# A decoder layer with routed experts: overflow code without branches, its loop moved, and expert matrices laid out in 16 KB rows

## The chip, the cores and the metric

The kernel runs on one core of one Trainium2 chip. The metric is the device time of one execution in microseconds (us). Of the core's parts, five matter here. PE (TensorE) multiplies matrices. DVE (VectorE) and ACT (ScalarE) do elementwise work, and they alone bring results from PE's accumulators (PSUM) to the on-chip memory (SBUF). SP (SyncE) issues nearly all loads from the chip's main memory (HBM), in the order of the program, on one queue that sixteen DMA engines serve. An instruction that has to wait on an engine or on SP holds back all that stand behind it there. POOL (GpSimd) does hardly anything in the part that is told of.

## What is computed

One decoder layer on 256 tokens of 1024 channels, all in float32: token mixers, a cross-attention, and then experts, each followed by a layer norm. The change touches the experts. A router gives each token its best 4 of 32 experts, with weights; each expert is a pair of matrices, w1 (1024 x 2048) and w2 (1024 x 1024):

```python
h = x_pad[tok] @ w1[e] + b1[e]
h_gate, h_up = h[:, :EXPERT_FF], h[:, EXPERT_FF:]
h_gate = jnp.minimum(h_gate, SWIGLU_LIMIT)
h_up = jnp.clip(h_up, -SWIGLU_LIMIT, SWIGLU_LIMIT)
act = h_gate * jax.nn.sigmoid(SWIGLU_ALPHA * h_gate) * (h_up + 1.0)
y = (act @ w2[e] + b2[e]).astype(F32)
return acc.at[tok].add(y * gate[:, None]), None
```

How many tokens an expert gets depends on the data. Every expert's 12 MB are used once, so all 403 MB are read in each execution.

## The kernel before, in words

The first third (mixers, cross-attention, router) is not touched. The experts follow, in 16 pairs; `prepare` (from line 1274) picks the tokens of a pair, CAP = 64 places for each expert, with matmuls against a selection (`gather`, line 1080: the tiles `xg1` to `xg15`, made one pair ahead, within the second expert of the pair before). Then, for each expert, in the order of the program on PE: w1 in four chunks (`expert_in`, line 1103), the activation on DVE and ACT (lines 1119 to 1123), four transposes (1130, 1131), w2 in two chunks (`expert_out`, 1144). After the second expert of a pair its results are added to the tokens (`add_out`, 1162 and 1163).

**The stream.** SP issues the chunks in the order in which they are used, six to an expert, 2 MB each (`echunk` and `fetch`, line 1023). They go to ten slots in turn (`RINGS`): a chunk can only be issued when PE is through with the chunk of ten places before. The names of the slots are tags of pools; one of them, `r3`, is the last of the ten. In memory an expert's matrices lie as they are given, row by row. A chunk of w1 is 256 rows of 8 KB and is loaded so that a partition takes two rows, p and p + 128; a chunk of w2 is 512 rows of 4 KB, of which a partition takes four. The matrices of the first third, `w_in`, are laid out by the host instead (in `layout`): each chunk as 128 partitions of 8 x 512 floats, 16 KB without a break.

**Overflow.** An expert may get more than 64 tokens. Before the experts start, the kernel looks for the expert with most tokens and swaps it with place PX = 17 (the order of the others stays; from place 2 on, SP reads from a table `idx_i` which expert's matrices to load). Places 65 to 96 of expert 17 are computed in a narrower form (`Extra`, 32 places, matmuls of 256 columns), with its matrices still in their slots: `overflow_in` behind its w1 and `overflow_out` behind its w2, each under a branch on the count (`tc.If`, line 1229 for the first) that PE, DVE and ACT read from the table `cnt_i`. Places beyond 96 have a loop within that branch. For all other experts stands `overflow_others` (from line 1237): if the highest count of the others is over 64, a loop over all experts loads matrices again, through POOL into slot `r3`, and computes the rest. It stands behind pair 8, that is behind expert 17, and all engines, SP too, load the count (line 1240) and take the branch (line 1241). In the data of these runs expert 17 has between 65 and 96 tokens, and no other has over 64: the first branch's work is done, the loop is skipped.

**The end.** Before expert 31, four accumulators are opened with the sum so far (`final`, line 1153), so that the last pair's results are added there; then the last layer norm, whose factors (`ln3`) SP loads behind all chunks, and four stores of the output.

Of the kernel before, what the change touches and what calls it, by code (L numbers as in the profile page):

```python
# [13 lines left out]
F32 = mybir.dt.float32  # L14
F32R = mybir.dt.float32r
BF16 = mybir.dt.bfloat16
I32 = mybir.dt.int32
U32 = mybir.dt.uint32
AF = mybir.ActivationFunctionType
OP = mybir.AluOpType  # L20
AX = mybir.AxisListType

P = 128
D = 1024
T = 256
NT = T // P
KT = D // P
E = 32
CAP = 64
# [4 lines left out]
NS = 2  # L34
PX = 17
# [12 lines left out]
def layer_kernel(ctx, tc, a, out, dbg=None):  # L48
    nc = tc.nc
# [954 lines left out]
    order = pool(ctx, "order")  # L1004

    Rp = order.tile([P, 2 * NT, E], F32, name="Rp")
    tab_i = order.tile([1, 2 * E + 2], I32, name="tab_i")
    cnt_i, idx_i = tab_i[:, 0:E + 2], tab_i[:, E + 2:]


    RINGS = [(ring2, "ring2")] * 3 + [(ring, "ring"), (ring3, "r0"), (ring3, "r1"), (ring, "ring"), (ring, "ring"),
# [3 lines left out]
    def slot(shape, name):  # L1015
        p, tag = RINGS[nslot[0] % len(RINGS)]
        nslot[0] += 1
        return p.tile(shape, F32, tag=tag, name=name)
# [10 lines left out]
            fetch(w[:, k:k + n], view[:, k:k + n])  # L1029
        return w  # L1030

    w1v = a["w_exp_in"][0].rearrange("e (c k p) n -> e c p k n", k=2, p=P)
    w2v = a["w_exp_out"][0].rearrange("e (c k p) n -> e c p k n", k=4, p=P)

    def of(v, e):
        return v[e] if isinstance(e, int) else v[bass.ds(e, 1)].rearrange("o c p k n -> (o c) p k n")
# [3 lines left out]

    def w2_views(e):
        return [([P, 4, D], of(w2v, e)[c]) for c in range(2)]

    BRANCH = (mybir.EngineType.PE, mybir.EngineType.DVE, mybir.EngineType.Activation)

    class Main:

# [11 lines left out]
    class Extra(Main):  # L1059
# [6 lines left out]
        bank = gate  # L1066
# [59 lines left out]
    def expert_turn(v, hu, at, nm):  # L1126
        W = v.W
        pt = v.bank("pt" + nm)
        for u in range(W // P):
            nc.tensor.transpose(pt[:, u * P:(u + 1) * P], hu[:, u * P:(u + 1) * P], ident)  # L1130
        nc.scalar.activation(at, pt[:, :W], AF.Copy, scale=0.5)  # L1131
# [18 lines left out]
    def final(t, half, alloc):  # L1150

        finals[t, half] = ps = alloc(f"pc{t}{half}_last")
        nc.tensor.matmul(ps, ident, acc[:, t, half * 512:half * 512 + 512], start=True, stop=False)

    def add_out(v, ct, y, rows, t, cols, nm):
        if finals:
# [48 lines left out]
    def extra_out(at, ct, w2, nm):  # L1205
        extra_add(expert_out(extra, at, w2, False, nm), ct, nm)
# [13 lines left out]
    def columns(e):  # L1220

        es = slice(e, e + 1)
        return Rp[:, 0:NT, es], Rp[:, NT:2 * NT, es], sel3p[:, es]

    def overflow_in(e, cnt, w1, w2):

        state = extra_tiles(f"x{e}")
        with tc.If(cnt > CAP):
            with tc.If(cnt > CAP + 32):
                for base in range(CAP + 32, T, 32):  # L1230
                    nm = f"x{e}_{base}"
                    extra_in(*columns(e), w1, base, *state, nm)
                    extra_out(*state, w2, nm)
            extra_in(*columns(e), w1, CAP, *state, f"x{e}")
        return state

    def overflow_others():

        pool = [mybir.EngineType.Pool]
        most = nc.values_load(cnt_i[0:1, E + 1:E + 2])  # L1240
        with tc.If(most > CAP):
            with tc.For_i(0, E) as i:
                here = bass.ds(i, 1)
                cnt = nc.values_load(cnt_i[0:1, here])
                with tc.If(cnt > CAP):
                    idx = nc.values_load(idx_i[0:1, here], engines=pool, min_val=0, max_val=E - 1)
                    own = md.tile([P, 2 * NT, 1], F32, tag="own", bufs=1, name="own")
                    sel = md.tile([3 * E, 1], BF16, tag="ownsel", bufs=1, name="ownsel")
                    nc.vector.tensor_copy(own, Rp[:, 0:2 * NT, here])
                    nc.vector.tensor_copy(sel, sel3p[:, here])  # L1250

                    def again(nm, shape, view):
                        w = ring3.tile(shape, F32, tag="r3", name="again" + nm)
                        nc.gpsimd.dma_start(w, view)
                        return w

                    def block(base):
                        nm = f"z{base}"
                        state = extra_tiles(nm)
                        extra_in(own[:, 0:NT], own[:, NT:], sel, (again(nm, s, w) for s, w in w1_views(idx)), base,  # L1260
                                 *state, nm)
                        py = expert_out(extra, state[0], (again(nm, s, w) for s, w in w2_views(idx)), False, nm)
                        extra_add(py, state[1], nm)

                    block(CAP)
                    with tc.If(cnt > CAP + 32):
                        for base in range(CAP + 32, T, 32):
                            block(base)

    def overflow_out(e, cnt, state, w2):  # L1270
        with tc.If(cnt > CAP):
            extra_out(*state, w2, f"x{e}")

    def prepare(pr):

# [55 lines left out]

    swap(few[0:1], few[0:1])
    nc.vector.tensor_copy(idx_i, few[0:1, 0])
    nc.vector.tensor_copy(cnt_i[0:1, E:E + 1], few[0:1, 1, PX:PX + 1])
    nc.vector.memset(few[0:1, 1, PX:PX + 1], 0.0)
    nc.vector.tensor_copy(cnt_i[0:1, 0:E], few[0:1, 1])
    nc.vector.tensor_reduce(kmax[0:1], few[0:1, 1], axis=AX.X, op=OP.max)
    nc.vector.tensor_copy(cnt_i[0:1, E + 1:E + 2], kmax[0:1])

# [22 lines left out]
    for pr in range(E // 2):  # L1364
        xg, og, rest = nxt
        Y = [md.tile([P, 512], F32, tag=f"Y{i}", bufs=1, name=f"Y{i}_{pr}") for i in range(2)]
        for i in range(2):
            e = 2 * pr + i
            w1 = []
            ex = e if e < NS else nc.values_load(idx_i[0:1, e:e + 1], engines=[mybir.EngineType.SP], min_val=0,  # L1370
                                                 max_val=E - 1)
            for c, (sh, view) in enumerate(w1_views(ex)):
                w1.append(echunk(sh, view, f"w1_{e}_{c}"))
                if e == 1 and c == 0:
                    acc_start(*acc_load())
            w2 = [echunk(sh, view, f"w2_{e}_{c}", 4 if e == E - 1 and c else 1)
                  for c, (sh, view) in enumerate(w2_views(ex))]
            nm = f"{e}"
            cnt = nc.values_load(cnt_i[0:1, E:E + 1], engines=BRANCH) if e == PX else None
            if e == E - 1:  # L1380
                for t, half in ((0, 0), (0, 1), (1, 0)):
                    final(t, half, bank)
            ps2 = expert_in(main, (sel3 if e < NS else sel3p)[:, e:e + 1], xg[:, :, i * CAP:(i + 1) * CAP], w1, nm, rest if e == 0 else None)
            hu = expert_swiglu(main, ps2, nm)
            if e == E - 1:
                final(1, 1, gbank)
            at = main.tile("at" + nm)
            state = overflow_in(e, cnt, w1, w2) if e == PX else None

            with tc.issue_after(nc.cur_bb.bb.instructions[-1]) if e == PX else ExitStack():  # L1390
                expert_turn(main, hu, at, nm)
            if i == 0:
                cts = [md.tile([P, T], F32, tag=f"ct{j}", bufs=1, name=f"ct{j}_{pr}") for j in range(2)]
                for j in range(2):
                    gate_rows(main, og[:, :, j:j + 2].rearrange("p t a s -> p t (a s)"), cts[j], f"{pr}_{j}")
            py = expert_out(main, at, w2, i == 1, nm)
            for j in range(2):
                rows = slice(j * CAP, (j + 1) * CAP)
                nc.scalar.activation(Y[j ^ i][rows, :], py[rows, :], AF.Copy)  # L1399
            if i == 1:  # L1400
                if pr + 1 < E // 2:
                    nxt = prepare(pr + 1)
            if e == PX:
                overflow_out(e, cnt, state, w2)
        for t in range(NT):
            for half in range(2):
                add_out(main, cts[half], Y[half], slice(0, P), t, slice(half * 512, half * 512 + 512), f"{half}_{pr}")

        if pr == PX // 2:
            overflow_others()  # L1410

    ln3 = slot([P, 2, D], "ln3")
    nc.sync.dma_start(ln3[:, 0], a["ln3_g"].to_broadcast([P, D]))
    nc.sync.dma_start(ln3[:, 1], a["ln3_b"].to_broadcast([P, D]))
    st = md.tile([P, NT, 2, 6], F32, tag="ln_st", bufs=1, name="ln3st")
    for t in range(NT):
        for half in range(2):
# [13 lines left out]
def masks():  # L1431
# [5 lines left out]
    def level(s):  # L1437
# [5 lines left out]


_PLAIN = ["x", "positions", "w_diff_o", "w_gdn_o", "w_mix_o", "ln1_g", "ln1_b", "w_cq", "w_ck", "w_cv", "w_co",
          "ln2_g", "ln2_b", "w_router", "b_router", "w_exp_in", "b_exp_in", "w_exp_out", "b_exp_out", "ln3_g",
          "ln3_b"]


def layout(inputs):  # L1450
# [3 lines left out]
    arr["memT"] = fm(np.asarray(inputs["mem"])[0], T)  # L1454
    arr["ln2_T"] = fm(np.concatenate([inputs["ln2_g"], inputs["ln2_b"]]), 2)
    arr["masks"] = masks()
    cw = np.asarray(inputs["gdn_conv_w"])[0]
    w = np.asarray(inputs["w_in"])[0]
    c = lambda o, g: np.arange(o + 256 * g, o + 256 * g + 256)
# [34 lines left out]
```

## Time and profile before

| what | value |
|---|---|
| median of 3 runs | 1528.34 us (1526.82 to 1529.77) |
| the profiled execution | 1527.18 us, of which its span in the profile 1525.5 us |
| PE busy | 1396.3 us, 92% of the span |
| DVE, ACT busy | 577.1 us (38%), 427.3 us (28%) |
| DMA | 480.21 MB in 91290 packets, 315 GB/s on average |

The page of the profile shows the share of busy time, the span in 40 slices, the DMA queues, the chain of work that ended last, and the costliest groups of instructions. Behind it stands the whole trace, which answers questions by line, tile, wait and stretch of time. An engine's "busy" for PE overlaps from one matmul to the next, so that 92% does not tell by itself whether PE is the bound; for that the waits are read. In the lists, "a <- b" after a wait means that a waited until b was done; names as PEq or SPq mean the engine's own queue of instructions; x16 is a count.

### The profile page before, as it was taken

The numbers are of one execution on the slowest core, as the hardware profiler recorded it, in microseconds if no ns is written. First come the engines' busy times: TensorE is split into PE (matmuls) and PEld (weight loads), VectorE is DVE, ScalarE is ACT, GpSimd is POOL, SyncE is SP. The second block draws the span as 40 slices with busy tenths as digits, with TensorE's granted clock in tenths as the row PEclk, the third lists the DMA queues.
The fourth block names the chain that finished last, engine by engine and source line by source line (L and its number), as shares of the span: only waits on it lengthen the run. The fifth ranks groups of instructions, "written<-read, shape, count | busy, mean of one in ns | idle before, by whom it ended". The sixth has DMA issues, their size and how long they took to land. (4 is left out here: it accounts for less than half of the span.)

```text
span 1525.5 us, 21509 instructions
## 1 busy us (share of the span) xinstructions
PE 1396.3 (92%) x8749; PEld 778.6 (51%) x8750; DVE 577.1 (38%) x1434; ACT 427.3 (28%) x925; POOL 8.8 (1%) x25
## 2 busy tenths in 40 slices
PE   7999999999999999999999999978689889899895
PEld 6788978799988633333333333323223323323331
DVE  6587869667875532112112112111112112112113
ACT  6575757665574311101101101100001101101111
POOL 0000000000000000000000000000000000000000
PEclk9999999999999999999999999997899999999998
DMA  7243334266854899999999999990799999999995
GB/s 278 96 167 112 111 112 148 75 225 206 304 215 159 318 404 418 418 416 416 418 418 416 417 417 418 416 389 2 291 418 417 418 415 418 418 417 415 418 418 219
DMA packets 91290, 480.21 MB, mean 315 GB/s; under 512 B 4336, under 2 KB 6928, under 8 KB 56144
## 3 DMA queue, kind: packets, MB, share of 16 engines
q1 hardware_dynamic: 90368, 475.72, 78.0%
q0 software_dynamic: 816, 3.04, 0.7%
q8 instruction: 71, 1.16, 0.3%
q14 instruction: 35, 0.29, 0.1%
HBM read 477.69 MB, written 1.05 MB: 314 GB/s over the span
## 5 line engine op out<-in xcount | busy, mean ns | idle before, releaser
L1103 PE MATMUL pgt<-w,xg 128*64 128x512 f32 x1024 | 250.6, 602 | 36.3 <-DMA w<-in_w_exp_in_dram 36.3
L1144 PE MATMUL py<-w,at 128*64 128x512 f32 x1024 | 242.5, 623 | 14.7 <-ACT at L1131 14.7
L1103 PE MATMUL pup<-w,xg 128*64 128x512 f32 x1024 | 248.6, 598 | 0.0
L1119 DVE TENSOR_SCALAR hg<-pgt 128x512 f32<-128x512 f32 x32 | 22.1, 692 | 511.4 <-PE pgt L1103 511.4
L1103 PEld LDWEIGHTS pgt<-w,xg 128*64 128x64 f32 x1024 | 71.6, 137 | 191.6 <-issue 135.3
L1103 PEld LDWEIGHTS pup<-w,xg 128*64 128x64 f32 x1024 | 75.6, 139 | 149.2 <-issue 149.2
L1120 ACT ACTIVATE th<-hg 128x512 f32<-128x512 f32 x32 | 20.1, 629 | 469.7 <-DVE hg L1119 469.7
L1144 PEld LDWEIGHTS py<-w,at 128*64 128x64 f32 x1024 | 72.2, 142 | 154.2 <-issue 129.7
L1399 ACT ACTIVATE Y<-py 64x512 f32<-64x512 f32 x64 | 37.9, 592 | 180.4 <-PE py L1144 180.0
L1162 PE MATMUL pc<-Y,ct 128*128 128x512 f32 x120 | 55.4, 604 | 2.7 <-ACT Y L1399 2.7
L1131 ACT ACTIVATE at<-pt 128x512 f32<-128x512 f32 x32 | 19.1, 597 | 94.9 <-PE pt L1130 94.9
L1163 DVE TENSOR_TENSOR acc<-acc,pc 128x512 f32<-128x512 f32 x60 | 41.1, 685 | 8.2 <-PE pc L1162 6.5
L1097 PEld LDWEIGHTS <-sel3p 96*64 96x64 bf16 (+1 forms) x128 | 10.5, 109 | 52.3 <-issue 52.3
L1097 PE MATMUL pup<-b,sel3p 96*64 96x512 bf16 x60 | 12.2, 389 | 25.4 <-DVE hu L1122 25.4
L1162 PEld LDWEIGHTS pc<-Y,ct 128*128 128x128 f32 x120 | 21.6, 189 | 26.9 <-issue 14.8
L334 DVE SCALAR_TENSOR_TENSOR u<-ps_g,feat,u 128x255 f32<-128x255 f32 (+2 forms) x72 | 33.1, 474 | 0.3
L1130 PE MATMUL pt<-ident,hu 128*128 128x128 f32 x128 | 21.5, 290 | 10.2 <-DVE hu L1123 10.2
L1121 DVE SCALAR_TENSOR_TENSOR hg<-th,hg 128x512 f32<-128x512 f32 x32 | 22.1, 692 | 22.3 <-ACT th L1120 22.3
L230 PE MATMUL ps_g<-xT,wg_0h 128*128 128x256 f32 x96 | 28.1, 293 | 0.9 <-ACT wg_0h L219 0.9
L232 PE MATMUL ps_g<-xT,wg_0l 128*128 128x256 f32 x96 | 28.1, 293 | 0.3 <-DVE wg_0l L220 0.3
L231 PE MATMUL ps_g<-xT,wg_0h 128*128 128x256 f32 x96 | 28.0, 292 | 0.0
L230 PE MATMUL ps_g<-xT,wg_1h 128*128 128x256 f32 x96 | 27.8, 290 | 0.0
(944 smaller groups left out, 2535.5 us busy)
## 6 DMA issues: line engine op xcount, KB each, us to landing
w<-in_w_exp_in_dram SPq DMA_DIRECT2D x128, 2048.0 KB, 25.8
w<-in_w_exp_out_dram SPq DMA_DIRECT2D x63, 2048.0 KB, 31.0
w_g<-in_w_in_dram SPq DMA_DIRECT2D x7, 2048.0 KB, 7.7
w_d<-in_w_in_dram SPq DMA_DIRECT2D x4, 2048.0 KB, 7.8
w_gt<-in_w_in_dram SPq DMA_DIRECT2D x4, 2048.0 KB, 7.8
w_dv<-in_w_in_dram SPq DMA_DIRECT2D x2, 2048.0 KB, 12.2
w_diffo<-in_w_diff_o_dram SPq DMA_DIRECT2D x2, 2048.0 KB, 11.7
w_gdno<-in_w_gdn_o_dram SPq DMA_DIRECT2D x2, 2048.0 KB, 8.3
```

The source lines that it names most:

```text
L230: nc.tensor.matmul(ps, h[:, kk, :], src[0][:, k, :], start=k == 0, stop=False)
L231: nc.tensor.matmul(ps, h[:, kk, :], src[1][:, k, :], start=False, stop=False)
L232: nc.tensor.matmul(ps, l[:, kk, :], src[0][:, k, :], start=False, stop=k == KT - 1)
L334: m1 = nc.vector.scalar_tensor_tensor(y[:, sh:], ps[:, :T - sh], convw[:, blk, tau:tau + 1], y[:, sh:], op0=OP.mult, op1=OP.add)
L1097: nc.tensor.matmul(ps[j * n:(j + 1) * n, :W], sel, b1[:, i * D + j * W:i * D + (j + 1) * W], start=True, stop=False)
L1103: nc.tensor.matmul(ps[j * n:(j + 1) * n, :W], xg[:, 2 * c + kk, :], w[:, kk, i * D + j * W:i * D + (j + 1) * W], start=False, stop=c == 3 ...
L1119: nc.vector.tensor_scalar(hg, pgt, 7.0, None, op0=OP.min)
L1121: nc.vector.scalar_tensor_tensor(hg, th, 1.0, hg, op0=OP.add, op1=OP.mult)
L1144: nc.tensor.matmul(py[j * n:(j + 1) * n, :W], at[:, k % U, (k // U) * n:(k // U + 1) * n], w[:, kk, hf * W:(hf + 1) * W], start=k == 0, st ...
L1162: nc.tensor.matmul(pc, ct[rows, t * P:(t + 1) * P], y[rows], start=True, stop=True)
L1163: nc.vector.tensor_tensor(acc[:, t, cols], acc[:, t, cols], pc, op=OP.add)
L1399: nc.scalar.activation(Y[j ^ i][rows, :], py[rows, :], AF.Copy)
```

## The change

Three things are done at once.

The overflow of expert 17 (`overflow_in`, and `extra_out` in place of `overflow_out`) is now always computed, for places 65 to 96, without a branch; the loads of its count on PE, DVE and ACT are gone. Places beyond 96 are left to the loop: the count of expert 17 in the table is set to 0 unless it is over 96, and positions up to 96 are cleared on DVE before the loop.

`overflow_others` is moved from behind pair 8 to just before the matmuls of expert 31, behind the issue of all chunks and of `ln3`, whose loads are moved up for that. Its loads go to the slot that is next in turn instead of `r3`, and its branch gets a new argument, `preferred_fallthrough_block=False`. The matmuls of expert 31 are held behind the opening of its accumulators.

The host lays `w_exp_in` and `w_exp_out` out so that in each chunk a partition's data is one run of 16 KB. The bytes and the slots of a chunk stay the same.

```diff
-    tab_i = order.tile([1, 2 * E + 2], I32, name="tab_i")
-    cnt_i, idx_i = tab_i[:, 0:E + 2], tab_i[:, E + 2:]
+    tab_i = order.tile([1, 2 * E + 1], I32, name="tab_i")
+    cnt_i, idx_i = tab_i[:, 0:E + 1], tab_i[:, E + 1:]
...
-    w1v = a["w_exp_in"][0].rearrange("e (c k p) n -> e c p k n", k=2, p=P)
-    w2v = a["w_exp_out"][0].rearrange("e (c k p) n -> e c p k n", k=4, p=P)
+    w1v, w2v = a["w_exp_in"], a["w_exp_out"]
...
-    def overflow_in(e, cnt, w1, w2):
+    def overflow_in(e, w1):
 
         state = extra_tiles(f"x{e}")
-        with tc.If(cnt > CAP):
-            with tc.If(cnt > CAP + 32):
-                for base in range(CAP + 32, T, 32):
...
-            extra_in(*columns(e), w1, CAP, *state, f"x{e}")
+        extra_in(*columns(e), w1, CAP, *state, f"x{e}")
         return state
 
     def overflow_others():
 
         pool = [mybir.EngineType.Pool]
-        most = nc.values_load(cnt_i[0:1, E + 1:E + 2])
-        with tc.If(most > CAP):
+        nc.vector.scalar_tensor_tensor(Rp[:, 0:NT, PX], Rp[:, 0:NT, PX], float(CAP + 32), Rp[:, 0:NT, PX],
+                                       op0=OP.is_gt, op1=OP.mult)
+        most = nc.values_load(cnt_i[0:1, E:E + 1])
+        with tc.If(most > CAP, preferred_fallthrough_block=False):
             with tc.For_i(0, E) as i:
...
                     def again(nm, shape, view):
-                        w = ring3.tile(shape, F32, tag="r3", name="again" + nm)
+                        p, tag = RINGS[nslot[0] % len(RINGS)]
+                        w = p.tile(shape, F32, tag=tag, name="again" + nm)
                         nc.gpsimd.dma_start(w, view)
                         return w
...
-    def overflow_out(e, cnt, state, w2):
-        with tc.If(cnt > CAP):
-            extra_out(*state, w2, f"x{e}")
...
-    nc.vector.tensor_copy(cnt_i[0:1, E:E + 1], few[0:1, 1, PX:PX + 1])
-    nc.vector.memset(few[0:1, 1, PX:PX + 1], 0.0)
+    own = few[0:1, 1, PX:PX + 1]
+    nc.vector.scalar_tensor_tensor(own, own, float(CAP + 32), own, op0=OP.is_gt, op1=OP.mult)
...
-            cnt = nc.values_load(cnt_i[0:1, E:E + 1], engines=BRANCH) if e == PX else None
             if e == E - 1:
+                ln3 = slot([P, 2, D], "ln3")
+                nc.sync.dma_start(ln3[:, 0], a["ln3_g"].to_broadcast([P, D]))
+                nc.sync.dma_start(ln3[:, 1], a["ln3_b"].to_broadcast([P, D]))
+                overflow_others()
                 for t, half in ((0, 0), (0, 1), (1, 0)):
-                    final(t, half, bank)
...
+                    begun = final(t, half, bank)
+
+            with tc.issue_after(begun.ins) if e == E - 1 else ExitStack():
+                ps2 = expert_in(main, (sel3 if e < NS else sel3p)[:, e:e + 1], xg[:, :, i * CAP:(i + 1) * CAP], w1, nm,
+                                rest if e == 0 else None)
...
-            state = overflow_in(e, cnt, w1, w2) if e == PX else None
-
-            with tc.issue_after(nc.cur_bb.bb.instructions[-1]) if e == PX else ExitStack():
-                expert_turn(main, hu, at, nm)
+            state = overflow_in(e, w1) if e == PX else None
+            expert_turn(main, hu, at, nm)
...
             if e == PX:
-                overflow_out(e, cnt, state, w2)
+                extra_out(*state, w2, f"x{e}")
...
-        if pr == PX // 2:
-            overflow_others()
-
-    ln3 = slot([P, 2, D], "ln3")
...
+    for n, c, k in (("w_exp_in", 4, 2), ("w_exp_out", 2, 4)):
+        w = np.asarray(inputs[n])[0]
+        arr[n] = np.ascontiguousarray(w.reshape(E, c, k, P, w.shape[2]).transpose(0, 1, 3, 2, 4))
```

More of the change, by code (lines that the diff above doesn't have):

```diff
@@ L1042, in w2_views @@
         return [([P, 4, D], of(w2v, e)[c]) for c in range(2)]
-    BRANCH = (mybir.EngineType.PE, mybir.EngineType.DVE, mybir.EngineType.Activation)
     class Main:
@@ L1152, in final @@
         finals[t, half] = ps = alloc(f"pc{t}{half}_last")
-        nc.tensor.matmul(ps, ident, acc[:, t, half * 512:half * 512 + 512], start=True, stop=False)
+        return nc.tensor.matmul(ps, ident, acc[:, t, half * 512:half * 512 + 512], start=True, stop=False)
     def add_out(v, ct, y, rows, t, cols, nm):
@@ L1223, in columns @@
         return Rp[:, 0:NT, es], Rp[:, NT:2 * NT, es], sel3p[:, es]
-    def overflow_in(e, cnt, w1, w2):
+    def overflow_in(e, w1):
         state = extra_tiles(f"x{e}")
-        with tc.If(cnt > CAP):
-            with tc.If(cnt > CAP + 32):
-                for base in range(CAP + 32, T, 32):
-                    nm = f"x{e}_{base}"
-                    extra_in(*columns(e), w1, base, *state, nm)
-                    extra_out(*state, w2, nm)
-            extra_in(*columns(e), w1, CAP, *state, f"x{e}")
+        extra_in(*columns(e), w1, CAP, *state, f"x{e}")
         return state
@@ L1333, in layer_kernel @@
     nc.vector.tensor_copy(idx_i, few[0:1, 0])
-    nc.vector.tensor_copy(cnt_i[0:1, E:E + 1], few[0:1, 1, PX:PX + 1])
-    nc.vector.memset(few[0:1, 1, PX:PX + 1], 0.0)
+    own = few[0:1, 1, PX:PX + 1]
+    nc.vector.scalar_tensor_tensor(own, own, float(CAP + 32), own, op0=OP.is_gt, op1=OP.mult)
     nc.vector.tensor_copy(cnt_i[0:1, 0:E], few[0:1, 1])
     nc.vector.tensor_reduce(kmax[0:1], few[0:1, 1], axis=AX.X, op=OP.max)
-    nc.vector.tensor_copy(cnt_i[0:1, E + 1:E + 2], kmax[0:1])
+    nc.vector.tensor_copy(cnt_i[0:1, E:E + 1], kmax[0:1])
     def acc_load():
@@ L1378, in layer_kernel @@
             nm = f"{e}"
-            cnt = nc.values_load(cnt_i[0:1, E:E + 1], engines=BRANCH) if e == PX else None
             if e == E - 1:
+                ln3 = slot([P, 2, D], "ln3")
+                nc.sync.dma_start(ln3[:, 0], a["ln3_g"].to_broadcast([P, D]))
+                nc.sync.dma_start(ln3[:, 1], a["ln3_b"].to_broadcast([P, D]))
+                overflow_others()
                 for t, half in ((0, 0), (0, 1), (1, 0)):
-                    final(t, half, bank)
-            ps2 = expert_in(main, (sel3 if e < NS else sel3p)[:, e:e + 1], xg[:, :, i * CAP:(i + 1) * CAP], w1, nm, rest if e == 0 else None)
+                    begun = final(t, half, bank)
+            with tc.issue_after(begun.ins) if e == E - 1 else ExitStack():
+                ps2 = expert_in(main, (sel3 if e < NS else sel3p)[:, e:e + 1], xg[:, :, i * CAP:(i + 1) * CAP], w1, nm,
+                                rest if e == 0 else None)
             hu = expert_swiglu(main, ps2, nm)
@@ L1407, in layer_kernel @@
                 add_out(main, cts[half], Y[half], slice(0, P), t, slice(half * 512, half * 512 + 512), f"{half}_{pr}")
-        if pr == PX // 2:
-            overflow_others()
-    ln3 = slot([P, 2, D], "ln3")
-    nc.sync.dma_start(ln3[:, 0], a["ln3_g"].to_broadcast([P, D]))
-    nc.sync.dma_start(ln3[:, 1], a["ln3_b"].to_broadcast([P, D]))
     st = md.tile([P, NT, 2, 6], F32, tag="ln_st", bufs=1, name="ln3st")
@@ L1445 @@
 _PLAIN = ["x", "positions", "w_diff_o", "w_gdn_o", "w_mix_o", "ln1_g", "ln1_b", "w_cq", "w_ck", "w_cv", "w_co",
-          "ln2_g", "ln2_b", "w_router", "b_router", "w_exp_in", "b_exp_in", "w_exp_out", "b_exp_out", "ln3_g",
+          "ln2_g", "ln2_b", "w_router", "b_router", "b_exp_in", "b_exp_out", "ln3_g",
           "ln3_b"]
```

## The prediction

> **What bounds the kernel now.** I read the page first, for the stage in which the time lies, and then asked the expert stage three things: what PE waits for, how long one pair of experts takes, and what the DMA queue waits for.
>
> The page's 40 slices are 38.1 us each; the last two rows are the busy share of the DMA engines and what they moved.
>
> ```profile
> span 1525.5 us, 21509 instructions
> ...
> DMA  7243334266854899999999999990799999999995
> GB/s 278 96 167 112 111 112 148 75 225 206 304 215 159 318 404 418 418 416 416 418 418 416 417 417 418 416 389 2 291 418 417 418 415 418 418 417 415 418 418 219
> ```
>
> From slice 14 on the experts' matrices stream at 415 to 418 GB/s, except for one slice (1030 to 1068 us) in which 2 GB/s moved. A full DMA row suggests a DMA-bound stage with a hole. It is only half true. The waits of PE between 570 and 972 us, longest first, begin with
>
> ```profile
> PE pup L1097 <- DVE hu L1122: 11.8, 14, 0.8
> ```
>
> (11.8 us in 14 waits), and none of the listed waits is for a DMA. In that stretch PE is the bound and the full DMA is only prefetching. How long a pair of experts takes PE is read from the gathers of line 1080, of which each pair makes one: the two numbers before the semicolon are the first and last start.
>
> ```profile
> L1080 PE MATMUL xg1p<-oh,x x32: 275/275/377, 573.2 to 580.5; 128*128 128x128 f32 x32
> ...
> L1080 PE MATMUL xg7p<-oh,x x32: 275/275/377, 914.5 to 921.9; 128*128 128x128 f32 x32
> L1080 PE MATMUL xg8p<-oh,x x32: 275/275/377, 970.6 to 977.9; 128*128 128x128 f32 x32
> ...
> L1080 PE MATMUL xg15p<-oh,x x32: 275/275/377, 1444.9 to 1452.2; 128*128 128x128 f32 x32
> ```
>
> From xg1 to xg8 are seven pairs in 970.6 - 573.2 = 397.4 us, 56.8 a pair (the last of them 56.1). From xg8 to xg15 are again seven pairs, but 474.3 us. The second half loses 76.9 us. Where?
>
> Later, PE does wait for DMA, so the starts of its matmuls tell when chunks (2 MB each) landed. In this timeline the bracket is the idle time before, and its cause.
>
> ```profile
> 1192.11 1.94 PE L1103 MATMUL pgt<-w,xg 128*64 128x512 f32 x8 [1.34 <-DMA w<-in_w_exp_in_dram]
> ...
> 1247.34 1.94 PE L1103 MATMUL pgt<-w,xg 128*64 128x512 f32 x8 [1.32 <-DMA w<-in_w_exp_in_dram]
> 1249.10 1.89 PE L1103 MATMUL pup<-w,xg 128*64 128x512 f32 x8
> 1252.31 1.94 PE L1103 MATMUL pgt<-w,xg 128*64 128x512 f32 x8 [1.32 <-DMA w<-in_w_exp_in_dram]
> ```
>
> 1192.11 and 1252.31 are the last chunk of w1 of two odd experts, one pair (12 chunks) apart: 60.20 us, 5.02 a chunk. Two chunks of w1 (pieces of 8 KB) are 4.97 apart, 1247.34 to 1252.31. Eight of w1 leave (60.20 - 39.8) / 4 = 5.10 for one of w2 (pieces of 4 KB). So DMA needs 60.2 us a pair and PE 56.8; PE is behind at first, has caught up by 1020 us, and after that DMA is the bound. The last wait before the hole and the first after it (start, duration):
>
> ```profile
> 1020.69 1.94 PE L1103 MATMUL pgt<-w,xg 128*64 128x512 f32 x8 [1.35 <-DMA w<-in_w_exp_in_dram]
> 1085.94 3.68 PE L1103 MATMUL pgt<-w,xg 128*64 128x512 f32 x8 [10.66 <-DMA w<-in_w_exp_in_dram]
> ```
>
> The first is the last w1 chunk of expert 17, the second the first of expert 18, with no chunk landing for w1 in the 65 us between them. The issues of SP's queue, its wait and the branch of line 1241 say why:
>
> ```profile
> 992.66 14.91 SPq L1023 DMA_DIRECT2D w<-in_w_exp_out_dram  x2
> 1077.81 2.75 SPq L1023 DMA_DIRECT2D w<-in_w_exp_in_dram  x4
> SPq L1023 <- PEq L1241: 60.9, 1, 60.9
> L1241 SPq COMPARE_BRANCH  x1: 53/53/53, 1015.9 to 1015.9; - x1
> L1241 PEldq COMPARE_BRANCH  x1: 3775/3775/3775, 1073.9 to 1073.9; - x1
> ```
>
> SP itself takes the branch of overflow_others at 1015.9, but its next load reuses slot r3, which the skipped loop's own loads also name, so it waits 60.9 us until PE has come to the same branch at 1073.9. PE comes late because it first does the overflow of expert 17. By then the ring is empty.
>
> **The change, part by part.** *The move of overflow_others.* At its new place SP has issued all expert chunks and ln3, and the slots that the loop names have no later user, so nothing that streams is queued behind the branch. The hole goes. What is late next is PE, with its own work.
>
> *The overflow of expert 17, now without branches.* Its work stays, and now lies on PE, the bound. The same work in the trace of before, and the granted clock (the number before the DMA share) in two stretches of it:
>
> ```profile
> 1030.95 1.93 PE L1189 MATMUL xsx<-x,ohx 128*32 128x256 f32 x16 [5.14 <-DVE ohx L1180]
> ...
> 1041.78 1.04 PE L1103 MATMUL pupx<-w,xgx 128*32 128x256 f32 x16
> 1042.64 1.04 PE L1103 MATMUL pgtx<-w,xgx 128*32 128x256 f32 x16
> ...
> 1047.04 3.66 PE L1144 MATMUL pyx<-w,atx 128*32 128x256 f32 x64 [0.29 <-ACT atx L1131]
> 1051.25 0.70 PE L1162 MATMUL pc0x<-yx,ctx 32*128 32x256 f32 x4 [0.55 <-ACT yx L1211]
> ...
> 1057.00 0.90 PE L1130 MATMUL pt<-ident,hu 128*128 128x128 f32 x3
> 1029.40:1039.50 10.10, 7.90 (x68) 3.69 (x72) 1.90 (x6) 0.39 (x1) 0.00 (x0) 0.50 0.02 5
> 1053.30:1057.00 3.70, 3.60 (x10) 1.91 (x9) 1.93 (x5) 0.00 (x0) 0.00 (x0) 0.50 0.00 0
> ```
>
> Bound from above: all of it with its waits, 1057.00 - 1030.95 = 26.1 us; the half clock in the two stretches (7.90 and 3.60 us of PE) costs half of that at most, so about 20.4 at full clock. From below: the matmuls alone, other work filling every wait. Sixteen are 0.86 apart (1041.78 to 1042.64), there are eight such groups for w1 and one for xsx, 7.8; pyx 3.7; four groups of pc0x at 0.70, 2.8; fourteen small transposes and biases at a tenth of a us (between 0.86 / 16 = 0.05 and 0.70 / 4 = 0.18), 1.5: 15.8, less 0.8 if they fill the wait for hu that an expert of the main work has on PE anyway (11.8 / 14): 15.0. I take 18, the middle, since program order puts the block where the main expert waits but its own chain through ACT and DVE stays.
>
> *Removed:* the branch of line 1229 and the loads of the count, in the 65 us that go.
>
> *The branch before expert 31.* PE loads the count, compares, and goes on. At least 0.1 us (SP's took 53 ns); at most PE's 3.8 us of before, and about 1 for bias products that can no longer be drawn ahead: 5. I take 2, nearer to the low end, as the new argument asks for the layout in which the branch is not taken when there is no overflow. [...]
>
> *The layout.* Pieces of 16 KB are not in the experts' trace, but w_in lies like that (128 partitions of 8 x 512 floats in a row). Its chunks are issued here, and this is what moved while they were alone in flight (clock, DMA share, GB/s last):
>
> ```profile
> 9.70 0.53 SPq L100 DMA_DIRECT2D w_g<-in_w_in_dram  x1
> 10.35 0.37 SPq L100 DMA_DIRECT2D w_dv<-in_w_in_dram  x1
> 15.00:20.00 5.00, 1.00 1.00 426
> 20.00:25.00 5.00, 1.00 1.03 436
> ```
>
> The mean of 431 GB/s is 2.097 MB / 431 = 4.87 us a chunk, against 4.97 and 5.10: 58.4 us a pair instead of 60.2. That is still over PE's 56.8, but PE never starts the stream level with it. Even if expert 17's last w1 chunk landed no earlier than 1020.7, the last w1 chunk of expert 31, 84 chunks on, would land at 1020.7 + 84 x 4.87 = 1429.8; PE wants it at about 1437 (below). So DMA stays ahead, by 7 us at worst, less some 2.5 for the delays in the stream that the first rival counts (84 x 0.03), and by about 17 if the 80-odd earlier chunks gain their 0.15 each (5.02 - 4.87). Held slots during the overflow cost nothing while PE is the bound. The layout's worth is thus small and hidden: it keeps DMA from taking over again.
>
> *The sum.* To xg8 nothing moves, as PE waited for no DMA: 970.6. Seven pairs at 56.8: 397.4. Overflow 18, branch 2. From xg15 to the end before: 1525.5 - 1444.9 = 80.6, with this one wait for DMA in it,
>
> ```profile
> PE pgt L1103 <- DMA w<-in_w_exp_in_dram: 0.9, 1, 0.9
> 1494.69 1.94 PE L1103 MATMUL pgt<-w,xg 128*64 128x512 f32 x8 [0.95 <-DMA w<-in_w_exp_in_dram]
> ```
>
> so 79.7. Span: 970.6 + 397.4 + 18 + 2 + 79.7 = 1467.7, against 1525.5. (The last 30.8, from 1494.69, are the tail, so PE wants that chunk at 1436.9.) The profiled execution took 1527.2, 1.7 over its span and 1.1 below the median of 1528.3, within the runs' 1526.8 to 1529.8. Forecast: 1469.4, a gain of 58.
>
> **The rivals.** *The new layout moves nothing faster, and DMA takes over.* With no hole but the old pace (1494.69 - 1085.94 = 408.8 us for 81 chunks, 5.05 each, all delays included), the last w1 chunk lands at 1020.7 + 84 x 5.05 = 1444.6; with 30.8 and 1.7 that is 1477. For it: the mean of 431 rests on two windows of 5 us. Against it: the step from 4 KB to 8 KB pieces already gave 0.13 us a chunk. Chance 0.13.
>
> *The branch at expert 31 stalls PE and halves its clock.* Before, the 5 us stand of PE at line 1229 ran into 10.1 us at a clock of 0.50. The same there: 3.8 more than the compare, 5 for the clock: about 7 over my 2, 1476. Against it: the flag, and PE's work right behind it. Chance 0.14.
>
> *Slower: the stride.* Partitions of one chunk now start 16 KB apart, where those of w1 were 8 KB apart in two sweeps. If the memory serves equal steps badly, each chunk takes longer on all of the stream, about 173 chunks from slice 14 on. It decides from the point at which the 50 us that a stream-bound version gains (1527 - 1477) are eaten: 50 / 173 = 0.29 us a chunk, 5.34 us, under 393 GB/s. [...] Chance 0.02.
>
> *The hole stays in part,* if the slots held by the overflow, or some wait that the new code adds on SP, empty the ring again: up to the old one, so 1480 to 1527. The ring holds ten chunks and PE is behind by several, so 0.05.
>
> **How the numbers follow.** My forecast, PE-bound, has 0.66. Its own range: overflow 15.0 to 20.4 (3.0 less, 2.4 more), branch 0.1 to 5 (1.9 less, 3 more), pairs at 56.1 like the last (4.9 less for seven) or at half a us more (3.5): 1459.6 to 1478.3. With the first two rivals, at 1476 and 1477 and some us around them, 1458 to 1484 holds over 8 in 10. A measurement of this kernel can tell a change of about 0.2%, 3 us, from none. All cases but the stride and the worst of the hole are faster: 0.97; 0.01 the same; 0.02 slower.
>
> **What would show it.** Right: no slice without DMA; xg8 at about 971 and xg15 at about 1386; no or few waits of PE for w after 1020; w chunks 4.9 us apart; most of the DMA packets at 16 KB. The overflow is sized by xg8 to xg9 less 56.8. Wrong: waits of PE for DMA all along the second half (first rival), a gap at expert 31 with a low clock behind it (second), chunks over 5.1 us apart (third), or a slice below 300 GB/s about 1030 us (fourth). That xg8 moves by more than 3 us would also be a fault of mine: I count the first half as PE's alone.

## The result and the profile after

| kernel | median, us | range, us | ratio to before, with 95% interval |
|---|---|---|---|
| before | 1527.62 | 1526.82 to 1529.77 | 1 |
| changed | 1476.87 | 1475.38 to 1477.97 | 0.9665 (0.9648 to 0.9682) |

The change saves 50.7 us, 3.3%; the forecast was 1469.4, 58 less. The profiled execution took 1475.38 us, its span 1473.7. First its page: the span, the DMA rows of the 40 slices (36.8 us each) and the packets.

```profile
span 1473.7 us, 21484 instructions
...
DMA  7243333354866689999999999999999999999980
GB/s 280 108 147 141 114 117 115 116 176 172 283 227 233 235 345 430 427 427 428 428 428 427 426 429 428 428 426 429 427 427 428 427 428 427 428 428 427 427 362 28
DMA packets 50713, 480.20 MB, mean 326 GB/s; under 512 B 4336, under 2 KB 6928, under 8 KB 23888
```

The slice with 2 GB/s is gone, and between the slices in which it starts and ends the stream runs at 426 to 430 GB/s instead of 415 to 418. The bytes are the same in 50713 packets instead of 91290. What PE waited for from 570 us to the end (us in total, times, longest):

```profile
PE pup L1094 <- DVE hu L1119: 22.8, 27, 0.8
PE py L1141 <- ACT at L1128: 13.9, 31, 0.7
PE pt L1127 <- DVE hu L1120: 11.3, 29, 1.8
PE pc_last L1150 <- issue: 6.6, 1, 6.6
PE pc L1159 <- ACT Y L1393: 2.7, 13, 0.2
PE pc_last L1155 <- ACT Y L1393: 0.7, 1, 0.7
```

That is the whole list, and no wait in it is for a DMA: after the change PE is the bound all through the experts. One line is new, 6.6 us before `pc_last`, which are the products that open the accumulators at expert 31. The gathers (line 1077 now; first and last start before the semicolon):

```profile
L1077 PE MATMUL xg1p<-oh,x x32: 275/275/377, 573.7 to 581.0; 128*128 128x128 f32 x32
...
L1077 PE MATMUL xg8p<-oh,x x32: 275/275/377, 971.7 to 979.0; 128*128 128x128 f32 x32
L1077 PE MATMUL xg9p<-oh,x x32: 275/275/377, 1035.3 to 1042.6; 128*128 128x128 f32 x32
L1077 PE MATMUL xg10p<-oh,x x32: 275/275/377, 1097.8 to 1105.1; 128*128 128x128 f32 x32
L1077 PE MATMUL xg11p<-oh,x x32: 275/275/377, 1153.9 to 1161.2; 128*128 128x128 f32 x32
L1077 PE MATMUL xg12p<-oh,x x32: 275/275/377, 1211.6 to 1219.0; 128*128 128x128 f32 x32
...
L1077 PE MATMUL xg15p<-oh,x x32: 275/275/377, 1385.0 to 1392.3; 128*128 128x128 f32 x32
```

xg8 was forecast for 971 and came at 971.7, xg15 for 1386 and came at 1385.0. From xg15 to the end of the span are 1473.7 - 1385.0 = 88.7 us, where the sum had 79.7 + 2 = 81.7. So the stream and the overflow cost what was expected, or a little less, and the miss lies behind xg15, where the moved branch stands. Its instructions on PE's queue (duration min/median/max in ns, first and last start), and who waited for them:

```profile
L1234 PEldq COMPARE_BRANCH  x2: 95/3104/6114, 1416.8 to 1421.0; - x2
...
L1234 PEldq EVENT_SEMAPHORE  x2: 51/51/51, 1420.7 to 1420.8; - x2
...
  PE pc_last L1150: 6.6, 1
```

The matmuls around it, from the timeline of PE,

```profile
1413.51 7.09 PE L1141 MATMUL py<-w,at 128*64 128x512 f32 x32 [0.25 <-ACT at L1128]
1427.23 5.00 PE L1150 MATMUL pc_last<-acc,ident 128*128 128x512 f32 x6 [6.63 <-issue]
```

and two stretches of it, with the granted clock behind the busy times (0.63, 0.54):

```profile
1424.00:1427.00 3.00, 0.00 (x0) 0.00 (x0) 0.00 (x0) 0.00 (x0) 0.00 (x0) 0.63 0.99 397
1427.00:1432.00 5.00, 4.77 (x6) 1.85 (x6) 0.00 (x0) 0.00 (x0) 0.00 (x0) 0.54 0.75 297
```

The compare at 1416.8 falls through in 95 ns, as the new argument asks. But there are two jumps at that line. The second starts at 1421.0, behind two semaphores that come right after PE's last matmul (1413.51 + 7.09 = 1420.60), and takes 6.11 us, in which PE does nothing. Then the clock is at about half until 1432. PE's instructions in the compiled program show where the second jump is from (not a view of the profile; waits for semaphores are left out of it). With the argument, the way around the loop's code is a jump of its own, right behind the compare:

```
 L1233 TENSOR_LOAD tab_i
 L1234 COMPARE_AND_BRANCH
 L1234 UNCONDITIONAL_BRANCH
 L1235 COMPARE_AND_BRANCH
```

Without the argument that third instruction stands behind the loop's code instead, where there is nothing left to jump over. So the branch of the compare is not taken, and a jump over the same code is taken all the same.

### The profile page after: what moved, and what is told of

Same layout as the page of the kernel before. It is cut to its first block, busy times and chain, and to the rows that moved or that the text cites. A ratio compares the mean times of both kernels' runs of the same rounds, so it can differ in the third digit from the quotient of the medians.

```text
span 1473.7 us, 21484 instructions
## 1 busy us (share of the span) xinstructions
PE 1385.1 (94%) x8749; PEld 775.8 (53%) x8750; DVE 576.9 (39%) x1434; ACT 427.4 (29%) x925; POOL 8.8 (1%) x25
## 2 busy tenths in 40 slices
DMA packets 50713, 480.20 MB, mean 326 GB/s; under 512 B 4336, under 2 KB 6928, under 8 KB 23888
## 5 line engine op out<-in xcount | busy, mean ns | idle before, releaser
L1141 PE MATMUL py<-w,at 128*64 128x512 f32 x1024 | 242.9, 622 | 13.9 <-ACT at L1128 13.9
L1100 PE MATMUL pgt<-w,xg 128*64 128x512 f32 x1024 | 246.9, 597 | 0.0
L1100 PE MATMUL pup<-w,xg 128*64 128x512 f32 x1024 | 244.4, 592 | 0.0
L1271 DVE TENSOR_TENSOR oh<-Rp,iota_s 128x128 f32<-128x128 f32 x30 | 7.4, 288 | 53.0 <-PE xg2p L1077 3.7
```

The lines of the kernel that those rows point to most:

```text
L1100: nc.tensor.matmul(ps[j * n:(j + 1) * n, :W], xg[:, 2 * c + kk, :], w[:, kk, i * D + j * W:i * D + (j + 1) * W], start=False, stop=c == 3 ...
L1141: nc.tensor.matmul(py[j * n:(j + 1) * n, :W], at[:, k % U, (k // U) * n:(k // U + 1) * n], w[:, kk, hf * W:(hf + 1) * W], start=k == 0, st ...
```

## The experiments

Theory: the time after the change is PE's; the miss is the branch at expert 31, about 9 us instead of 2. Rivals: the miss is spread over the stream, or over the last experts whatever the branch does; and the layout is worth next to nothing beside the moves.

### The branch: left out, and without its argument

`no_loop` leaves out `overflow_others` (the loop over the other experts, which this data skips). `no_flag` keeps it without the argument. `changed_again` is the changed kernel once more, on the same chip.

```diff
 no_loop:
-                overflow_others()
 no_flag:
-        with tc.If(most > CAP, preferred_fallthrough_block=False):
+        with tc.If(most > CAP):
```

> The changed kernel once more, beside the other kernels of this set. Both theories: about 1476 us, ratio to before 0.966.

> The changed kernel without overflow_others: the places of other experts beyond 64, of which these data have none, are left out, and with them the branch. Theory (the branch costs 6 us of stand and about 3 of half clock on PE, the bound): 1466 to 1468. Rival (the second half is slow because the clock dips, and the branch is hidden): 1474 to 1477.

> The changed kernel with the argument preferred_fallthrough_block taken away; nothing else differs. Theory (PE is the bound all through, and the stand at expert 31 is the second jump of this layout, which PE's queue only takes after it has waited for its own matmuls, so that nothing hides the fetch): with one branch, taken at once while PE still works off w2 of expert 30, most of the 6 us are hidden and the clock does not halve, 1467 to 1470. Rival (the code has to be fetched either way, with the loads of expert 31 in front of it): 1474 to 1477, as with the flag.

Measured: `changed_again` 1476.77 us (0.9667, 0.9653 to 0.9680); `no_loop` 1466.60 (0.9604, 0.9591 to 0.9617); `no_flag` 1472.41 (0.9642, 0.9625 to 0.9660). The last gather in `no_loop`, whose span is 1465.1 us:

```profile
L1077 PE MATMUL xg15p<-oh,x x32: 275/275/377, 1385.2 to 1392.6; 128*128 128x128 f32 x32
```

From xg15 to the end are 1465.1 - 1385.2 = 79.9 us, where the sum had 79.7 without a branch. The branch costs 88.7 - 79.9 = 8.8 us of the span, 1476.77 - 1466.60 = 10.2 by the medians. In the profiled execution of `changed_again` it costs 10.0 (span 1476.4, xg15 at 1386.5): PE stands for 7.0 us instead of 6.6, and the clock is at half for 10.2 us instead of 6.8. The theory holds and the first rival is out.

`no_flag` fell between what the theory and the rival gave. Its branch, its matmuls and the stretch before:

```profile
L1234 PEldq COMPARE_BRANCH  x1: 6597/6597/6597, 1421.1 to 1421.1; - x1
```

```profile
1416.21 8.70 PE L1141 MATMUL py<-w,at 128*64 128x512 f32 x32 [0.25 <-ACT at L1128]
1428.12 2.81 PE L1150 MATMUL pc_last<-acc,ident 128*128 128x512 f32 x6 [3.22 <-PEq L1234]
```

```profile
1412.00:1420.00 8.00, 5.96 (x24) 2.15 (x22) 2.83 (x6) 1.23 (x2) 0.00 (x0) 0.79 1.01 429
```

One jump only, taken, of 6.60 us: the rival was right that the jump stays as long. It starts at 1421.1 while PE still works off w2 until 1416.21 + 8.70 = 1424.91, so 3.8 us of it are hidden and PE stands for 3.2; the six `pc_last` behind it run at full clock, 2.81 us instead of 5.00. From xg15 to the end it takes 1472.4 - 1387.7 (xg15 of this run) = 84.7, 4.8 over `no_loop`: the stand of 3.2 and 1.6 for a dip of the clock in the expert before (py 8.70 where it is 7.09 at full clock), which has nothing to do with the branch. The argument does harm here: not because its jump is longer, but because that jump only begins when PE's own matmuls are done. By the times alone this is not quite settled, as the intervals of the two ratios overlap (0.9653 and 0.9660); the traces show it.

### The layout and the moves apart

`old_rows` has the moves with the old layout, `old_rows_no_loop` the same without `overflow_others`, and `rows_alone` is the kernel before with the new layout only.

```diff
 old_rows, against the changed kernel (old_rows_no_loop also leaves out overflow_others()):
-    w1v, w2v = a["w_exp_in"], a["w_exp_out"]
+    w1v = a["w_exp_in"][0].rearrange("e (c k p) n -> e c p k n", k=2, p=P)
+    w2v = a["w_exp_out"][0].rearrange("e (c k p) n -> e c p k n", k=4, p=P)
```

For `rows_alone` the same lines of the kernel before are changed the other way round; in each case the host's layout goes with them.

> The moves alone: the changed kernel with the experts' matrices as they are given, pieces of 8 and 4 KB. Theory (DMA takes over near 1010 us at 5.05 us a chunk, lands the last w1 chunk at about 1445 against 1443 in the changed kernel, and PE's stand at expert 31 is then spent in waiting for it): 1477 to 1480, so that the layout is worth 1 to 3 us beside the moves. Rival (a faster stream pays by its rate on each of the last 84 chunks): 84 x 0.15 us, 13 us, about 1489.

> The layout alone: the kernel before with the experts' matrices in rows of 16 KB, overflow and loop as they were. Theory (PE is the bound up to expert 17, DMA behind the hole): the 3.7 us of waits for DMA just before the hole go, and behind it 81 chunks at 4.92 (4.89 and some delays) in place of 5.05 save 10 us; 1513 to 1516. Rival (with the hole in place the faster stream only stands idle longer): 1524 to 1528.

> The moves without the layout, and without overflow_others (its work, of which these data have none, is left out). Theory (DMA is the bound from about 1005 us on, so that what PE saves at the branch is lost again in waiting for w1): the last w1 chunk lands at about 1446 as in the run with the branch, plus 30.8 and 1.7: 1478 to 1480, some 12 us over the same without the branch in rows of 16 KB. Rival (branch and layout simply add up): 1486.0 - 10.2 = 1475.8.

Measured: `old_rows` 1485.96 (0.9733, 0.9719 to 0.9746); `rows_alone` 1514.19 (0.9904, 0.9889 to 0.9919); `old_rows_no_loop` 1478.87 (0.9675, 0.9661 to 0.9688).

`rows_alone` came as expected, 13.9 us under the kernel before. Its two parts can't be read as well as the sum: the profiled execution (1518.67 us) is the slowest of its four, and though PE's waits for DMA ahead of the hole are gone in it, the stretch behind the hole is 6.6 us shorter, not 10 (1517.0 - 1084.0 from the first chunk there to the end, against 1525.5 - 1085.94). After the hole PE waits for many of its chunks there, so the starts of its matmuls tell when w1 chunks land in the new layout:

```profile
1114.11 1.94 PE L1102 MATMUL pgt<-w,xg 128*64 128x512 f32 x8 [1.47 <-DMA w<-in_w_exp_in_dram]
...
1128.80 1.94 PE L1102 MATMUL pgt<-w,xg 128*64 128x512 f32 x8 [1.25 <-DMA w<-in_w_exp_in_dram]
```

The second row is the third chunk after the first: 14.69 us, 4.90 each; the estimate from `w_in` was 4.87, the old pieces took 4.97 and 5.10.

`old_rows` is neither what the theory nor what the rival gave. Its waits for DMA, the last two of them, and where it comes to the last w1 chunk of expert 31:

```profile
PE pgt L1101 <- DMA w<-in_w_exp_in_dram: 8.1, 7, 1.4
```

```profile
1379.14 1.94 PE L1101 MATMUL pgt<-w,xg 128*64 128x512 f32 x8 [1.34 <-DMA w<-in_w_exp_in_dram]
1384.16 1.94 PE L1101 MATMUL pgt<-w,xg 128*64 128x512 f32 x8 [1.37 <-DMA w<-in_w_exp_in_dram]
...
1456.27 1.88 PE L1101 MATMUL pgt<-w,xg 128*64 128x512 f32 x8
```

1384.16 is the last w1 chunk of expert 29, taken as it lands. One pair of chunks on, at the old pace of 60.2 us, the last w1 chunk of expert 31 lands at 1444.4, just where the prediction's first rival had it (1444.6). But PE wants it only at 1456.27. From expert 25 to 29 PE waited for the stream (8.1 us in 7 waits), and then it stood at the branch. The two delays add up, since they lie one behind the other; the rival's 1477 and my 1477 to 1480 took the larger of the two. Without the branch the same layout gives 1478.87, inside 1478 to 1480, but not by the way that was expected: PE's waits for DMA there (12.9 us in 11 times) end with expert 29, and it does not wait for w1 of expert 31 at all.

So the new layout is worth 13.9 us alone, 9.2 beside the moves (1485.96 - 1476.77) and 12.3 beside them without the branch (1478.87 - 1466.60, from two chips, on which the kernel before differs by 0.6). The moves alone bring 41.5 (1527.45, the kernel before on that chip, less 1485.96). The second rival is out: the layout decides who is the bound in the last third. How the 41.5 divides between the loop's new place, its new slot and the overflow without branches is not shown; no run changes one of them by itself.

### The branch put behind expert 31's w1

If the stand lies where PE has to wait for the activation in any case (0.83 us for `hu`, then its transposes), it might cost less. `loop_behind_w1` puts the call and the four openings of the accumulators there, without the argument, and no longer holds expert 31's matmuls behind them; `loop_behind_w1_flag` does so with it.

```diff
             if e == E - 1:
                 ln3 = slot([P, 2, D], "ln3")
...
-                overflow_others()
-                for t, half in ((0, 0), (0, 1), (1, 0)):
-                    begun = final(t, half, bank)
...
             hu = expert_swiglu(main, ps2, nm)
             if e == E - 1:
+                overflow_others()
+                for t, half in ((0, 0), (0, 1), (1, 0)):
+                    final(t, half, bank)
                 final(1, 1, gbank)
```

> The changed kernel without the flag, and with overflow_others and the opening of the four accumulators moved behind w1 and the activation of expert 31. Theory (a fetch costs what neither PE's queued matmuls nor a wait of its own hides): PE has 3 to 4 us of matmuls queued there, no load is in flight any more, and PE waits for the activation in any case; 1464 to 1468, as without the loop. Rival (the branch costs its 4 to 6 us wherever it stands): 1471 to 1473.

> The same place with the flag. Theory (the second jump of this layout waits for PE's own matmuls first): the fetch, about 4 us with no load in flight, lies in the open beside the activation alone, which covers some 2 of it: 1467 to 1471, 2 to 5 us over the same without the flag. Rival (the flag makes no difference): the same as without it.

Measured: 1469.72 (0.9624, 0.9611 to 0.9637) and 1471.11 (0.9627, 0.9613 to 0.9641). The first lies between its theory and its rival. These two are the fastest kernels of the study that still do the whole work, the first 7 us under the changed one, but 3 over `no_loop`. The branch of the first, and PE around it:

```profile
L1234 PEldq COMPARE_BRANCH  x1: 6086/6086/6086, 1429.1 to 1429.1; - x1
```

```profile
1431.02 1.89 PE L1100 MATMUL pup<-w,xg 128*64 128x512 f32 x8
1435.61 5.37 PE L1150 MATMUL pc_last<-acc,ident 128*128 128x512 f32 x8 [2.70 <-PEq L1234]
```

PE stands for 2.7 us, which the activation would have cost it in part, but then the openings come in the open and at half clock, 5.37 us for eight products. The jump is hardly shorter than in `no_flag` (6.09 against 6.60), and the expectation's premise fails: loads are still in flight, 274 and 229 GB/s in the jump's first two us. In `loop_behind_w1_flag` the jump over the loop's code begins later, at 1435.3, when the experts' loads are through (10 GB/s from 1436 to 1440), and takes 3.46 us; that is the "about 4 us with no load in flight" of its expectation. Between the two kernels of this pair the intervals overlap, so here the argument makes no difference that these runs can tell.

All of PE's jumps over the loop's code in the kept traces fall into these two classes. Six begin with the experts' loads in flight and take 6.0 to 6.6 us (6.00 in `no_overflow`, 6.09, 6.11 and 6.60 in `loop_behind_w1`, the changed kernel and `no_flag`); three begin with none in flight and take 3.36 (`rows_alone`), 3.46 and 3.78 us (the kernel before, in its hole). The packets that DMA moved during the jump differ; first the kernel before from 1073.9 to 1077.7, then the changed kernel from 1420.9 to 1427.1:

```profile
q8 instruction: 1, 0.02, 2.3%
q14 instruction: 1, 0.01, 0.8%
```

```profile
q1 hardware_dynamic: 413, 2.50, 98.6%
q8 instruction: 1, 0.02, 1.1%
q14 instruction: 2, 0.02, 0.8%
```

In the hole nothing moves but two packets of instructions. In each of the nine jumps the trace has one packet of 16 KB on queue q8; it takes 1.0 to 1.4 us, and the jump ends 1.4 to 1.5 us after it has landed. What differs is when it starts: 1.0 us after the jump begins where no load is in flight (1074.90 in the kernel before), 3.4 to 4.1 us after it beside the stream (1424.44 in the changed kernel, 3.48 us after 1420.95). I read this as a wait for code, which starts 2.4 to 3.1 us later beside the experts' loads. That the packet is the jump's code and queues behind the loads is argued; that it starts later beside them, and that the jump ends that soon after it, is shown.

### The overflow work left out

`no_overflow` leaves out the work for places 65 to 96 of expert 17, to size it.

```diff
-            state = overflow_in(e, w1) if e == PX else None
...
-            if e == PX:
-                extra_out(*state, w2, f"x{e}")
```

> Left out: the work for places 65 to 96 of expert 17 (overflow_in and extra_out); everything else as in the changed kernel. Theory: this work costs 14 us of PE (xg8 to xg9 took 70.05 us where a clean pair takes 56.08), because a part of it fills waits of the main experts, and nothing behind it has slack, so all of it shows in the time: 1476.8 - 14 = about 1463, with xg8 to xg9 at 56 to 58. Rival A: the 18 us of the prediction were right and the rest was lost elsewhere, or leaving it out removes waits as well: 1457 to 1459. Rival B: DMA is so near behind PE in the second half that PE, 14 us earlier at expert 31, waits for w there: 1468 or more, with waits of PE for w in the listing. Chunks landed 9 to 30 us ahead of their use, so B would show only if the lead at expert 31 is under 14.

Measured: 1466.53 us (0.9601, 0.9588 to 0.9614), 10.3 us under the changed kernel. (The 70.05 of the expectation counts one pair from the start of its w1; by the gathers the work is spread over xg8 to xg10.) Two of its gathers, its only waits for DMA, and from its timeline the waits of expert 17 and of two chunks:

```profile
L1077 PE MATMUL xg8p<-oh,x x32: 275/275/377, 974.0 to 981.4; 128*128 128x128 f32 x32
...
L1077 PE MATMUL xg10p<-oh,x x32: 275/275/377, 1087.9 to 1095.2; 128*128 128x128 f32 x32
```

```profile
PE pgt L1100 <- DMA w<-in_w_exp_in_dram: 2.2, 2, 1.2
```

```profile
1024.45 0.41 PE L1094 MATMUL pup<-b,sel3p 96*64 96x512 bf16 x2 [0.84 <-DVE hu L1119]
1025.18 0.65 PE L1127 MATMUL pt<-ident,hu 128*128 128x128 f32 x4 [0.32 <-DVE hu L1120]
1026.52 3.65 PE L1141 MATMUL py<-w,at 128*64 128x512 f32 x16 [0.69 <-ACT at L1128]
...
1360.92 1.94 PE L1100 MATMUL pgt<-w,xg 128*64 128x512 f32 x8 [0.95 <-DMA w<-in_w_exp_in_dram]
1365.82 1.94 PE L1100 MATMUL pgt<-w,xg 128*64 128x512 f32 x8 [1.25 <-DMA w<-in_w_exp_in_dram]
```

The work itself is as the theory has it. The changed kernel takes 126.1 us from xg8 to xg10, this one 113.9, of which 1.7 are a dip of the clock (below): 126.1 - 112.2 = 13.9. But the whole is not 14 faster. Some 330 us later PE, now ahead, meets the stream and waits 2.2 us for two chunks (1360.92 and 1365.82, 4.90 apart): rival B of the expectation, at a smaller size. The rest of the gap between 14 and 10.3 is not settled. The clock seems to have a part in it: the median of the granted clock over this kernel's runs is 0.981, over the changed kernel's 0.985, and in this profiled run xg8 already came 2.3 us later than in the changed kernel's, before the work in question. So the stream is the next bound, and it lies less than 14 us under PE.

How the work comes to 13.9 is seen in the changed kernel's timeline:

```profile
1007.13 1.89 PE L1100 MATMUL pgt<-w,xg 128*64 128x512 f32 x8
1008.84 1.89 PE L1100 MATMUL pup<-w,xg 128*64 128x512 f32 x8
1010.66 1.07 PE L1100 MATMUL pgtx<-w,xgx 128*32 128x256 f32 x16
1011.55 1.05 PE L1100 MATMUL pupx<-w,xgx 128*32 128x256 f32 x16
1012.52 1.94 PE L1100 MATMUL pgt<-w,xg 128*64 128x512 f32 x8
...
1030.34 1.07 PE L1141 MATMUL py<-w,at 128*64 128x512 f32 x2 [0.20 <-ACT at L1128]
```

Without its branch the overflow is no longer a block behind expert 17: each of its groups runs right behind the main one that uses the same chunk. Its w1 costs about 1.9 a chunk (1010.66 to 1012.52), and the waits that expert 17 has on PE without it, 0.84 + 0.32 + 0.69 = 1.85 us, have shrunk to 0.20.

## Why the prediction was right, and where it was off

Right, point by point: **the bound.** PE, not the full DMA row, set the pace before the hole, and sets it all the way after the change; xg8 came within 1.1 us. **The hole** was SP's wait for slot r3 and goes whole with the moves: no slice between the first and the last of the stream is under 426 GB/s. (In the prediction's rows the slices on either side of the hole, 389 and 291 GB/s, belong to it too.) **The layout** is worth 0.07 us a w1 chunk and, by the prediction's 5.10, 0.20 a w2 chunk, which keeps DMA ahead to the end. "Small and hidden" was too weak a word for it: without it PE waits for DMA from expert 25 on, and the time is 9 us longer. **The stride** of 16 KB costs nothing that these runs can show (4.90 us a chunk), and **no part of the hole** stayed.

The forecast's 1467.7 of span against 1473.7 breaks up so:

| term | forecast | measured | difference |
|---|---|---|---|
| to xg8 | 970.6 | 971.7 | +1.1 |
| seven pairs, without the overflow | 397.4 | 399.4 | +2.0 |
| overflow of expert 17 | 18 | 13.9 | -4.1 |
| from xg15 to the end, without the branch | 79.7 | 79.9 (`no_loop`) | +0.2 |
| branch at expert 31 | 2 | 8.8 | +6.8 |

The errors partly cancel: without the 4.1 us that the overflow came out cheaper, the span would have been 10 us over the forecast instead of 6.

**The step that failed is the branch.** Its price lay in the prediction, as the second rival: 3.8 us of stand and 5 us of half clock, "about 7 over my 2, 1476". That this sum meets the measured 8.8 so well is luck: the stand was 6.6 us and not 3.8, and the half clock cost 2.2 and not 5 (the six `pc_last` take 5.00 us instead of 2.81). The 3.8, which also bounded my own range, was read in the hole, where no load was in flight. I took 2, since "the new argument asks for the layout in which the branch is not taken". The argument was read as a promise about all jumps at that line; it only says which side the compare falls to. The way around the loop's code is jumped either way. The jumps over the loop's code are long on PE (6.11 us here, 6.60 and 6.09 in two variants, 3.78 in the kernel before), and the packet of instructions lands in each before it ends; that there would be no taken one was wrong. No run shows a branch there at the 2 us of the sum: in its place the runs show 8.8 us of span, 10.2 by the medians.

**The overflow** was mis-sized, and came out under my lower bound of 15.0. The list of its matmuls (15.8 us) was right. I let it fill 0.8 us of waits, one of the three waits that expert 17 has; it fills 1.65 of the 1.85, and its own chain through ACT and DVE, for which I went up to 18, is hidden by the main work it now runs between.

**The pairs** hold 2.0 us more through dips of the clock. Most pairs are either 56.1 us long (xg10 to xg11) or 57.7 (xg11 to xg12). In each of the longer ones the granted clock halves once, as here:

```profile
1204.00:1206.00 2.00, 1.06 (x6) 0.52 (x5) 0.95 (x2) 0.27 (x1) 0.00 (x0) 1.00 1.04 442
1206.00:1207.00 1.00, 0.62 (x2) 0.30 (x4) 0.00 (x0) 0.33 (x1) 0.00 (x0) 0.68 0.96 410
1207.00:1209.00 2.00, 2.00 (x7) 0.48 (x5) 0.00 (x0) 0.00 (x0) 0.00 (x0) 0.50 1.00 426
```

About 3.4 us at half clock cost 1.7. My mean of 56.8 a pair had fewer dips in it (397.4 - 7 x 56.1 = 4.7, not quite three) than the second half has (four pairs of 57.7 or 57.8). In each of the kept traces all changes of the granted clock (18 to 34; 25 in the kernel before, 19 in the changed one) lie on one grid with a step of 3.413 us, to within 3 ns, and the dips of these pairs are one window of it long. In the window before this dip PE was busy for 1.58 of 3.41 us (1202.94 to 1206.36), and for up to 2.0 before other dips of this length in the experts' stage. The busy time alone does not tell: in the changed kernel a window with 1.99 us of work (from 711.42) was followed by a dip, and one with 1.86 (from 909.39) was not.

In two runs the price of a wait went with its place on the grid. The stand of 2.7 us in `loop_behind_w1` lies whole in one window (1432.50 to 1435.90, PE busy for 0.70 us), and the clock halved behind it; the 3.2 us in `no_flag` are split over two (1422.90 to 1426.30 and on to 1429.70, busy for 2.00 and 1.58 us), and it did not. A pair with one dip, 57.8 us, is also nearly 17 windows long (58.0), so that the next pair meets the grid in nearly the same place; that this is why the last four dips before the branch come 58.0 us apart is argued and not tested.

The last 1.5 us of the 7.5 between 1469.4 and 1476.87 lie between the profiled execution, the fastest of its four, and their median.

## What to carry to other kernels

A skipped block costs a jump on every engine that takes part, and on the engine that is the bound that jump is a term of the sum (6.6 us of stand here), with the half clock behind it (2.2 us); whether a compare is called taken or not says nothing until all jumps at that line have been counted, and a price read where no load is in flight (3.8 us here) is too low beside a full stream (6.1). When a queue has a hole, ask who the bound will be once it is closed and how far the next one lies below: here PE and DMA were less than 14 us apart, so that savings on one of them did not show in full (13.9 us of overflow work left out gave 10.3). Delays that lie one behind the other on one engine add up, and the larger of two bounds is then too low an estimate.

## What the runs showed of the hardware that was not expected

- The jump over the loop's code takes 6.0 to 6.6 us on PE beside the experts' loads and 3.4 to 3.8 with none in flight, while the jumps of DVE, ACT and SP take under 0.1 (72, 50 and 53 ns in `no_flag`). In between lies the jump of line 1229 in the kernel before (4.2 us from 1026.1), during which the last loads before the hole run out (the last packet starts at 1030.3).
- In all kept traces the granted clock changes only at the steps of a grid of 3.413 us, whose first step lies at another place in each (1.91 us behind the span's start in the kernel before, 1.45 in the changed one).
- PE's queue reached the compare 3.8 us before its matmuls were done (1416.8 against 1420.6). The taken jump of `no_flag` in that place hid 3.8 of its 6.60 us; that of the changed kernel, behind a wait for PE's own matmuls, hid nothing of its 6.11.
- The size of the pieces still counts above 4 KB: 2 MB took 5.10 us in pieces of 4 KB (the remainder of one pair in the prediction), 4.97 in pieces of 8 KB (4.95 to 5.02 in the runs with the old layout) and 4.90 in pieces of 16 KB.
